# A hybrid decoder layer on one core: both projections by Strassen's identity, features in two halves, partial sums in DRAM

## The chip, the cores and the metric

The kernel runs on one core of a Trainium2 chip. The metric is the device time of one execution in microseconds, lower is better; a profiled execution also leaves a trace of every instruction on the core's engines: TensorE (PE, with its weight loads PEld), VectorE (DVE), ScalarE (ACT), GpSimd (POOL) and SyncE (SP), which issues nearly all DMAs.

## The reference

One layer over 1024 tokens of 2048 features, all in float32, batch 1:

```python
mod = silu(c) @ w_ada + b_ada                    # (2048) x (2048, 6144)
shift, scale, gate = split(mod, 3)
h = rms_norm(x, norm_gain) * (1 + scale) + shift
proj = h @ w_in                                  # (1024, 2048) x (2048, 8192)
q_sb, k_sb, v_sb, z_sb, q_r, k_r, v_r, z_r = split(proj, 8)   # 1024 columns each
# eight heads of 128: stick-breaking attention, strictly causal
qa, ka = rms_norm(q, q_gain), rms_norm(k, k_gain)             # per head
beta = sigmoid(qa . ka / sqrt(128))
A[t, s] = beta[t, s] * prod_{s < j < t} (1 - beta[t, j])
oa = (A @ v) * silu(z_sb)
# eight heads of 128: retention in chunks of 128 tokens
o[t] = sum_{s <= t} gamma_h ** (t - s) (rot(q_t) . rot(k_s)) v_s
ob = group_norm(o) * ret_gain * silu(z_r)
out = x + gate * (concat(oa, ob) @ w_out)        # (1024, 2048) x (2048, 2048)
```

The two projections are nearly all of the arithmetic.

## The kernel before

A float32 operand of a projection is split into two parts, a high one that TensorE's faster fp32r format holds exactly (ACT copy) and the rest (VectorE subtraction, line 121 for weights). A product of two operands is three matmuls (`mm3`, lines 132 to 135): high x high, low x high, high x low. PE's order is the program's (`manual_schedule`, line 61); the other engines' and the DMA queue's order is set by a scheduler, by priority and estimated readiness.

**Start (lines 218 to 450).** x is loaded by blocks of 128 tokens, scaled by its rows' root mean squares and transposed on PE. Sums of silu(c) w_ada run in chunks of 256 columns (`ada_sums`, line 273), on VectorE, ACT and POOL. The scale's chunks come first, the shift's later: until then h.T stands without its shift, and from that the z columns of seven retention heads are projected (`start_mm`) and spilled to DRAM; the shift's share in them is added later (`z_bias`, line 508).

**Input projection.** h.T stays in SBUF as 16 blocks of features by two halves of tokens, in two parts. `unit_t` (line 139) takes 128 columns of w_in: 16 blocks x 2 halves x 3 matmuls, 128 weights x 512 tokens, accumulated over all features in a PSUM bank a half. `unit_v` (line 156) takes 256 columns of values with h as the stationary operand: 256-wide matmuls whose result stands by tokens, as the heads need it. Weights are streamed in 256 KB tiles (`wchunk`, line 124).

**Heads.** The heads are tasks whose small products stand between the steps of the projection (`steady` calls `tick` after each six matmuls; a task says how many steps it waits). `qk_norm` (line 539) takes q and k from SBUF and works out their norms as 512-wide tiles with three Newton iterations (lines 556 to 561). `sb_attention` (line 581) takes blocks of 128 queries by 512 keys: sigmoids on ACT (619, 620), masks on POOL (622, 624), a running product on VectorE (632), a product (636), transposes on PE (649), splits (663, 664), products with the values. `ret_attention` (line 797): rotation of q and k (788 to 795), states (816, 822), scores (829, 831), values with their statistics (842 to 859), transposes and gating (866 to 872). Head outputs go to DRAM (`concat`).

**Output projection (`out_unit`, line 749).** Four groups of 512 columns of w_out over all 16 blocks of features, tokens in PSUM's partitions; the first group by halves of tokens while the last head ends. `finish` (line 940) multiplies by the gate and adds x (951, 952). The gate's sums run on VectorE during the retention heads (`gate_part`, line 484).

Of the kernel before, what the change touches and what calls it, by code (L numbers as in the profile page):

```python
# [29 lines left out]
SB_GAP = 3  # L30
NORM_GAP = 3
NORM_GAP2 = 6
SPLIT_GAP = 2
ZT = 1
BE = 3
TURN = 2
TURN_PRIO = 400
RT_ONE = False
ZB_GAP = 2
K0_WAIT = 8  # L40
NZ = 7
ADA_BUFS = 9
ADA_ACT = (2, 4, 7, 9, 12, 14)
SHIFT_GAP = 6
X_LOAD = {3: (4,), 5: (5,), 7: (6,), 8: (7,)}
X_STAT = {5: (4,), 7: (5,), 9: (6,), 10: (7,)}
X_TURN = 10
MOD_AT = 4
ENG = mybir.EngineType
MANUAL = (ENG.PE,)  # L50
LO_POOL = ()
RT_GAP = 5
# [3 lines left out]
def layer_kernel(ctx, tc, x, c, w_ada, b_ada, norm_gain, w_in, sb_q_gain, sb_k_gain, ret_norm_gain, w_out,  # L56
# [12 lines left out]
    concat = [dr.tile([P, S], F32, name=f"concat{f}") for f in range(KC)]  # L69
    gate_row = dr.tile([1, D], F32, name="gate_row")  # L70

# [1 line left out]
    ident = cons.tile([P, P], F32, name="ident")  # L73
    make_identity(nc, ident)
    ones = cons.tile([P, 32], F32, name="ones")
    nc.vector.memset(ones, 1.0)
    mean_r = cons.tile([P, P], F32R, name="mean_r")
    nc.vector.memset(mean_r.bitcast(F32), 1.0 / HD)

    c_sb = hp.tile([P, HALF], F32, tag="hl14_1", name="c_sb")[:, 0:16]  # L80
# [3 lines left out]

# [4 lines left out]
    cols = cons.tile([P, 58], F32, name="cols")  # L89
    rows = hp.tile([P, HALF], F32, tag="hl15_1", name="rows")  # L90
    nc.vector.memset(rows[:, 0:P], 0.0)
    nc.scalar.dma_start(rows[0:16, 0:P], norm_gain.rearrange("o (k p) -> (o k) p", p=P))
    nc.scalar.dma_start(rows[16:48, 0:P], b_ada[:, 0:2 * D].rearrange("o (k p) -> (o k) p", p=P))
    nc.scalar.dma_start(rows[48:49, 0:P], sb_q_gain)
    nc.scalar.dma_start(rows[49:50, 0:P], sb_k_gain)
    nc.scalar.dma_start(rows[50:58, 0:P], ret_norm_gain.rearrange("o (k p) -> (o k) p", p=P))
    rows_ps = ps.tile([P, P], F32, tag="C", name="rows_ps")
    nc.tensor.transpose(rows_ps, rows[:, 0:P], ident)
    nc.vector.tensor_copy(cols, rows_ps[:, 0:58])
    gain_c = cols[:, 0:16]  # L100
    shift_b = cols[:, 16:32]
    qg = cons.tile([P, 1], F32, name="qg")
    nc.vector.tensor_scalar(qg, cols[:, 48:49], 1.0 / math.sqrt(HD), None, op0=ALU.mult)
    kg = cols[:, 49:50]
    ret_g = cols[:, 50:58]

    def rsqrt_newton(y, m, u, iters=3):
        """y = m ** -0.5 from the exponent trick and Newton's iteration (u is room for a product)."""
        nc.vector.tensor_scalar(y.bitcast(I32), m.bitcast(I32), -0.5, RSQRT_MAGIC, op0=ALU.mult, op1=ALU.add)
        for _ in range(iters):  # L110
            nc.vector.tensor_tensor(u, y, y, op=ALU.mult)
            nc.vector.scalar_tensor_tensor(u, u, -0.5, m, op0=ALU.mult, op1=ALU.mult)
            nc.vector.scalar_tensor_tensor(y, u, 1.5, y, op0=ALU.add, op1=ALU.mult)

# [1 line left out]
    def split_w(raw, name, lo_eng=nc.vector):  # L116
        n = raw.shape[1]
        hi = wp.tile([P, HALF], F32R, tag="wh", name=f"wh_{name}")
        nc.scalar.activation(hi[:, 0:n], raw, AF.Copy)  # L119
        lo = wp.tile([P, HALF], F32R, tag="wl", name=f"wl_{name}")  # L120
        lo_eng.tensor_tensor(lo[:, 0:n], raw, hi[:, 0:n].bitcast(F32), op=ALU.subtract)  # L121
        return hi, lo

    def wchunk(parts, name, lo_eng=nc.vector):
        raw = wp.tile([P, HALF], F32, tag="wr", bufs=3, name=f"wr_{name}")
        for dst, src in parts(raw):
            nc.sync.dma_start(dst, src)
        return split_w(raw, name, lo_eng)

    w_in_k = w_in[0].rearrange("(k p) n -> p k n", p=P)  # L130

    def mm3(o, a_hi, a_lo, b_hi, b_lo, first, last):
        nc.tensor.matmul(o, a_hi, b_hi, start=first, stop=False)  # L133
        nc.tensor.matmul(o, a_hi, b_lo, start=False, stop=False)  # L134
        nc.tensor.matmul(o, a_lo, b_hi, start=False, stop=last)  # L135

    h_hi, h_lo = {}, {}  # by block of 128 features and half of the tokens

    def unit_t(col0, halves, name, lo_pool=()):
        """(w_in[:, col0:col0+128]).T @ h.T, 512 tokens a bank. Yields between its steps; returns the banks."""  # L140
        o = {hf: ps.tile([P, HALF], F32, tag="pj", bufs=4, name=f"pj_{name}_{hf}") for hf in halves}
        for kq in range(4):
            def parts(raw):
                yield raw.rearrange("p (k n) -> p k n", n=P), w_in_k[:, 4 * kq:4 * kq + 4, col0:col0 + P]
            with tc.high_priority(AHEAD):
                hi, lo = wchunk(parts, f"{name}_{kq}", nc.gpsimd if kq in lo_pool else nc.vector)
            for hf in halves:
                for k in range(4):
                    kc = 4 * kq + k
                    sl = slice(k * P, (k + 1) * P)  # L150
                    mm3(o[hf], hi[:, sl], lo[:, sl], h_hi[kc, hf], h_lo[kc, hf], kc == 0, kc == KC - 1)
                    if k % 2:
                        yield
        return o

    def unit_v(col0, name):
        """h @ w_in[:, col0:col0+256]: two heads' values, two blocks of tokens a bank."""
# [853 lines left out]
```

## Time and profile before

| | |
|---|---|
| device time, median of 3 | 2157.0 us (2154.09 to 2159.65) |
| span of the profiled execution | 2156.7 us |
| mean granted TensorE clock | 0.989 |
| PE / DVE / ACT / POOL busy | 2066.9 / 1212.4 / 744.9 / 340.0 us |
| DMA | 224.29 MB, mean 104 GB/s |

The page of the profile gives busy time by engine, forty slices of the span with the busy share in tenths, the chain of work that ended last, and groups of equal instructions with `xcount | busy us, mean ns | idle time before them and what ended it`. Matmuls are pipelined, so the mean durations of back-to-back ones overlap. A row of the windows gives, for a stretch, the busy time and instruction count of each engine, the granted clock, the DMA engines' share and GB/s. The profiled execution's own time is its span.

### The profile page before, as it was taken

To read this page: it belongs to the slowest core of one execution; us is meant where nothing else is said; L and a number is where in the kernel's file an instruction comes from. 1 tells how busy PE (TensorE), PEld (TensorE's weight loads), DVE (VectorE), ACT (ScalarE), POOL (GpSimd) and SP (SyncE) were. 2 spreads that over 40 slices of the span, in tenths; PEclk is the share of its full clock that TensorE was granted. 3 is DMA by queue.
4 is the path that set the end of the run, shared out by engine and by line. 5 is a ranking of instruction groups with operands and counts; after the bars stand their busy time and mean duration, and the time that the engine had idled before them with its cause. 6 is when DMAs were issued, how large, how long until landed. Compare 5 with 4: busy or idle time off the path is not lost.

```text
span 2156.7 us, 29735 instructions
## 1 busy us (share of the span) xinstructions
PE 2066.9 (96%) x11167; PEld 1771.6 (82%) x11167; DVE 1212.4 (56%) x2270; ACT 744.9 (35%) x1424; POOL 340.0 (16%) x475
## 2 busy tenths in 40 slices
PE   4878899999999999999999999999999999999998
PEld 3656779888988898888988988988988988688887
DVE  6999774477448653865386556556355146523132
ACT  6655442444235433543254222223232123311110
POOL 3654330111011201120111101011011010000000
PEclk9989999999999999999999999999999999999999
DMA  8847511221222112121212533433232124734132
GB/s 281 297 153 231 181 49 59 79 69 45 64 69 74 50 59 74 56 62 59 74 50 77 168 117 96 132 97 115 89 96 62 54 62 146 223 104 132 49 127 78
DMA packets 232404, 224.29 MB, mean 104 GB/s; under 512 B 12674, under 2 KB 187844, under 8 KB 232260
## 3 DMA queue, kind: packets, MB, share of 16 engines
q1 hardware_dynamic: 231872, 222.36, 32.8%
q8 instruction: 87, 1.43, 0.3%
q14 instruction: 57, 0.47, 0.1%
q10 hardware_dynamic: 388, 0.04, 0.0%
HBM read 194.03 MB, written 28.32 MB: 103 GB/s over the span
## 4 chain that ended last, share of the span: by engine, by line
PE 73%; DVE 13%; DMA 5%; issue 4%; ACT 3%; POOL 1%; ACTq 0%; SPq 0%; DVEq 0%; POOLq 0%
PE y L134 4%; PE y L135 4%; PE y L133 4%; PE pv_v L135 3%; PE pv_v L134 3%; PE pv_v L133 3%; PE pj_rq L133 3%; PE pj_rq L135 3%; PE pj_rq L134 3%; PE pj_rk L133 3%; PE pj_rk L135 3%; PE pj_rk L134 3%; PE pj_q L134 2%; PE pj_z L133 2%; PE pj_q L133 2%
## 5 line engine op out<-in xcount | busy, mean ns | idle before, releaser
L133 PE MATMUL pv_rv<-wh_rv,h_hi 128*128 128x256 f32 x512 | 146.5, 286 | 3.5 <-ACT wh_rv L119 3.5
L133 PE MATMUL y<-wh_o,c_hi 128*128 128x512 f32 x384 | 149.4, 389 | 0.0
L134 PE MATMUL y<-wl_o,c_hi 128*128 128x512 f32 x384 | 149.4, 389 | 0.0
L135 PE MATMUL y<-wh_o,c_lo 128*128 128x512 f32 x384 | 149.4, 389 | 0.0
L134 PE MATMUL pv_rv<-wl_rv,h_hi 128*128 128x256 f32 x512 | 146.1, 285 | 0.8 <-DVE wl_rv L121 0.7
L134 PE MATMUL pv_v<-wl_v,h_hi 128*128 128x256 f32 x512 | 144.9, 283 | 0.0
L133 PE MATMUL pv_v<-wh_v,h_hi 128*128 128x256 f32 x512 | 144.9, 283 | 0.0
L135 PE MATMUL pv_rv<-wh_rv,h_lo 128*128 128x256 f32 x480 | 136.4, 284 | 0.0
L135 PE MATMUL pv_v<-wh_v,h_lo 128*128 128x256 f32 x480 | 135.8, 283 | 0.0
L121 DVE TENSOR_TENSOR wl_o<-wr_o,wh_o 128x512 fp32r<-128x512 f32 x48 | 33.2, 692 | 180.3 <-ACT wh_o L119 180.3
L632 DVE TENSOR_TENSOR_SCAN om<-om 128x128 f32<-128x128 f32 (+2 forms) x96 | 96.2, 1002 | 43.6 <-POOL om L622 42.3
L119 ACT ACTIVATE wh_o<-wr_o 128x512 fp32r<-128x512 f32 x48 | 30.3, 632 | 220.7 <-PE y L135 216.3
L133 PEld LDWEIGHTS pv_rv<-wh_rv,h_hi 128*128 128x128 f32 x512 | 98.8, 193 | 4.9 <-ACT wh_rv L119 3.9
L133 PE MATMUL pj_rq<-h_hi,wh_rq 128*128 128x512 f32 x256 | 102.6, 401 | 0.3 <-ACT v L469 0.3
L133 PE MATMUL pj_rk<-h_hi,wh_rk 128*128 128x512 f32 x256 | 102.3, 400 | 0.0
L283 POOL TENSOR_TENSOR acc_p<-acc_p,ada 128x256 f32<-128x256 f32 x96 | 87.0, 907 | 96.9 <-ACT ada L282 68.0
L133 PE MATMUL pj_z<-h_hi,wh_z 128*128 128x512 f32 x256 | 101.3, 396 | 0.0
L133 PE MATMUL pj_q<-h_hi,wh_q 128*128 128x512 f32 x256 | 100.7, 393 | 0.0
L135 PE MATMUL pj_q<-h_hi,wl_q 128*128 128x512 f32 x256 | 100.6, 393 | 0.0
L134 PEld LDWEIGHTS pv_rv<-wl_rv,h_hi 128*128 128x128 f32 x512 | 98.9, 193 | 1.8 <-DVE wl_rv L121 1.6
L133 PE MATMUL pj_k<-h_hi,wh_k 128*128 128x512 f32 x256 | 100.2, 392 | 0.0
L135 PE MATMUL pj_rq<-h_hi,wl_rq 128*128 128x512 f32 x256 | 100.1, 391 | 0.0
(273 smaller groups left out, 5820.9 us busy)
## 6 DMA issues: line engine op xcount, KB each, us to landing
ada<-in_w_ada_dram SPq DMA_DIRECT2D x64, 512.0 KB
gr<-in_w_ada_dram SPq DMA_DIRECT2D x64, 256.0 KB
wr_o<-in_w_out_dram SPq DMA_DIRECT2D x48, 256.0 KB
x<-in_x_dram SPq DMA_DIRECT2D x32, 256.0 KB
wr_rz<-in_w_in_dram SPq DMA_DIRECT2D x32, 256.0 KB
wr_q<-in_w_in_dram SPq DMA_DIRECT2D x32, 256.0 KB
wr_k<-in_w_in_dram SPq DMA_DIRECT2D x32, 256.0 KB
wr_z<-in_w_in_dram SPq DMA_DIRECT2D x32, 256.0 KB
```

The source lines that it names most:

```text
L119: nc.scalar.activation(hi[:, 0:n], raw, AF.Copy)
L121: lo_eng.tensor_tensor(lo[:, 0:n], raw, hi[:, 0:n].bitcast(F32), op=ALU.subtract)
L133: nc.tensor.matmul(o, a_hi, b_hi, start=first, stop=False)
L134: nc.tensor.matmul(o, a_hi, b_lo, start=False, stop=False)
L135: nc.tensor.matmul(o, a_lo, b_hi, start=False, stop=last)
L283: nc.gpsimd.tensor_tensor(acc_p, acc_p, src, op=ALU.add)
L632: nc.vector.tensor_tensor_scan(rev, rev, rev, init, op0=ALU.mult, op1=ALU.bypass)
```

## The change

The new program splits tokens, features and columns in halves of pairs of blocks and takes Strassen's identity in Winograd's form: seven products of half-size blocks instead of eight, with sums of blocks ahead and behind. Names: A11, A12, A21, A22 are the left blocks (two halves of tokens by even and odd feature blocks), `S1` to `S4` their sums, the right blocks are B11 to B22 of the weights.

- Left operands: only half the features (8 of 16 blocks) are in SBUF at a time, as four pairs of blocks; for each of the seven combinations there are four tiles in two parts (`place`). The second half of h.T is held in DRAM (`xs`) and replaces the first at the end of the first stream (`gather`, `swap`).
- A `Group` is 256 columns by half the features: two loads of 512 KB, four sums of weights on VectorE, seven splits, seven products of 4 blocks x 3 matmuls (128 weights x 512 tokens), all with tokens along the width, values too. P1, P6, P5 and P3 accumulate in one bank, P7 and P4 in a second, P2 stands in a third; between them ACT copies the bank (`copied`) and VectorE adds (`added`).
- The input projection runs as two streams of 32 groups: the first half of the features, with partial sums written to DRAM (`part`), then the second half, which adds the loaded partial sums on POOL (line 237) or VectorE and writes the results to DRAM (`fin`). The output projection likewise: features of the stick-breaking heads, then of the retention heads (`ypart`).
- P3 and P4 of a group stand behind the first product of the next.
- Heads take q, k, v, z from DRAM. Values are transposed on PE (`turn_v`). The norm's means are worked out over 256 tokens at a time through single-buffered tiles, written to DRAM as a row, read back one number a token, and applied in the sigmoids' scale (q) and as a broadcast row (k).
- The stick-breaking heads run in the second input stream, the retention heads from its end into the first output stream. Head outputs go to DRAM; `mix_sums` makes S1 to S4 of them on POOL, and `take` loads the left tiles of the next stream behind the last use of the old ones, calling `tick` until the mixed tiles are written.
- All of w_ada is summed on VectorE: four blocks of scale and shift before the first product, the other four and the gate as a task in the first stream. The z columns need no later bias.
- The output is transposed back on PE (128 transposes) and added to x.

```diff
-    def unit_t(col0, halves, name, lo_pool=()):
-    def unit_v(col0, name):
...
+    def combine(a11, a12, a21, a22, new, sub):
+        s1, s2, s4 = (new(n) for n in ("S1", "S2", "S4"))
+        sub.tensor_tensor(s1, a21, a22, op=ALU.add)
+        sub.tensor_tensor(s2, s1, a11, op=ALU.subtract)
+        sub.tensor_tensor(a21, a11, a21, op=ALU.subtract)
+        sub.tensor_tensor(s4, a12, s2, op=ALU.subtract)
+        return {"A11": a11, "S3": a21, "S2": s2, "A12": a12, "S1": s1, "S4": s4, "A22": a22}
...
+        def product(self, p, bank, first):
+            with tc.high_priority(AHEAD):
+                src = self.right(p)
+                hi = wp.tile([P, NP, P], F32R, tag="wh", bufs=3, name=f"wh_{self.name}_{p}")
+                lo = wp.tile([P, NP, P], F32R, tag="wl", bufs=3, name=f"wl_{self.name}_{p}")
+                split(hi, lo, src)
+            for j in range(NP):
+                a_hi, a_lo = left[LEFT[p], j]
+                mm3(bank, hi[:, j, :], lo[:, j, :], a_hi, a_lo, first and j == 0, j == NP - 1)
+                if j % 2:
+                    yield
...
+    def copied(g, src, i, hf, name):
+        t = pp.tile([P, HALF], F32, tag="pt", bufs=PT, name=f"{name}_{g.name}")
+        gt = g.gate[i]
+        nc.scalar.activation(t, src, AF.Copy, scale=1.0 if gt is None else gt)
+        if g.seed is not None:
+            nc.gpsimd.tensor_tensor(t, t, old(g, i, hf), op=ALU.add)
+        return t
...
+        def second_half():
+            for j in range(NP, 2 * NP):
+                acc = yield from ada_sums(k1, "sg", NSG, "sg", (D + 256 * j, 256 * j), f"a{j}", 4)
+                yield 4
+                ada_mod(j, acc)
+            for i in range(4):
+                acc = yield from ada_sums(k1, "sg", NSG, "sg", (2 * D + 512 * i, 2 * D + 512 * i + 256), f"g{i}", 4)
+                yield 4
+                mod = over_partitions(acc, f"g{i}")
...
+        run(stream([Group(w_in_k, 0, 256 * i, f"e{i}", put=to_dram(part, 2 * i)) for i in range(32)], gather))
...
+    def qk_norm(h, pool):
+        for i, b in enumerate((h, NH + h)):
+            for qt in range(4):
+                sl = slice(qt * 256, (qt + 1) * 256)
+                sq = pool.tile([P, 256], F32, tag="n0", name=f"sq_{b}_{qt}")
+                nc.sync.dma_start(sq, fin[b][:, sl])
+                nc.scalar.activation(sq, sq, AF.Square)
+                shi = pool.tile([P, 256], F32R, tag="n1", name=f"shi_{b}_{qt}")
+                slo = pool.tile([P, 256], F32R, tag="n2", name=f"slo_{b}_{qt}")
+                split(shi, slo, sq)
+                yield PRO_GAP
+                ms = ps.tile([P, 256], F32, tag="A0", name=f"ms_{b}_{qt}")
+                nc.tensor.matmul(ms, mean_r, shi, start=True, stop=False)
+                nc.tensor.matmul(ms, mean_r, slo, start=False, stop=True)
+                row = pool.tile([P, 256], F32, tag="n0", name=f"row_{b}_{qt}")
+                nc.scalar.activation(row[0:1, :], ms[0:1, :], AF.Identity, bias=eps_c[0:1, :])
+                nc.sync.dma_start(msq[h][i:i + 1, sl], row[0:1, :])
...
+    def take(g):
+        def tell(n):
+            for j in range(NP):
+                while f"mix{g}_{j}" not in ready:
+                    tick()
+                    switch()
+                place(n, j, loaded(mix[g][j][n], f"c{g}_{n}_{j}"))
+        return tell
+
+    run2(stream(second, take(0)))
+    run2(stream([Group(w_out_k, 0, 256 * i, f"y{i}", gate=gates[2 * i:2 * i + 2], put=to_dram(ypart, 2 * i))
+                 for i in range(8)], take(1)))
+    drain()
...
+        run(stream([Group(w_out_k, 8, 256 * i, f"o{i}", seed=ypart[2 * i:2 * i + 2], gate=gates[2 * i:2 * i + 2],
+                          put=put_y(i), done=lambda i=i: start(finish(i), 2)) for i in range(8)]))
```

The prediction calls the four streams first (e), second (f), first output (y) and second output (o).

1216 lines of the change are left out of this document (541 added, 675 removed).

## The prediction

> **What bounds the kernel now.** I read the page first: busy shares, slices, the chain that ended last.
>
> ```profile
> span 2156.7 us, 29735 instructions
> PE 2066.9 (96%) x11167; PEld 1771.6 (82%) x11167; DVE 1212.4 (56%) x2270; ACT 744.9 (35%) x1424; POOL 340.0 (16%) x475
> ...
> PE   4878899999999999999999999999999999999998
> DVE  6999774477448653865386556556355146523132
> ...
> PE 73%; DVE 13%; DMA 5%; issue 4%; ACT 3%; POOL 1%; ACTq 0%; SPq 0%; DVEq 0%; POOLq 0%
> ```
>
> TensorE is busy 96% of the span and in every slice but the first five; the chain is 73% PE. VectorE (DVE) is the next engine, 56% on average but 6 to 9 tenths early on. Only fewer or shorter products can make this kernel much faster, as long as nothing that feeds them becomes later. Second, four stretches (PE, PEld, DVE, ACT and POOL busy with instruction counts, granted clock, DMA share, GB/s):
>
> ```profile
> 0.00:300.00 300.00, 232.05 (x982) 183.89 (x983) 246.90 (x437) 165.81 (x350) 139.69 (x141) 0.93 0.65 210
> 0.00:60.00 60.00, 30.00 (x129) 24.04 (x130) 42.63 (x97) 37.88 (x88) 24.46 (x33) 0.94 0.88 285
> 180.00:260.00 80.00, 68.59 (x287) 55.69 (x288) 71.71 (x109) 38.00 (x74) 35.74 (x37) 0.91 0.65 205
> 300.00:1180.00 880.00, 874.84 (x4950) 762.15 (x4950) 525.00 (x857) 358.26 (x698) 123.01 (x284) 1.00 0.20 63
> ```
>
> The start moves 285 GB/s and is held by DMA; around 200 us VectorE is 90% busy and PE waits (granted clock 0.91); the heads' 880 us run with PE 99% busy while VectorE has 525 us of work. This room on VectorE, 355 us, is what the change spends. Third, the timeline, for the pace of back-to-back products, since the mean durations in the groups overlap:
>
> ```profile
> 1507.33 0.28 PE L134 MATMUL pv_rv<-wl_rv,h_hi 128*128 128x256 f32 x1
> 1507.69 0.28 PE L134 MATMUL pv_rv<-wl_rv,h_hi 128*128 128x256 f32 x1
> 1509.10 0.39 PE L842 MATMUL op<-v,pT 128*128 128x128 f32 x2
> 1509.55 0.39 PE L842 MATMUL op<-v,pT 128*128 128x128 f32 x2
> ...
> 2140.07 0.39 PE L133 MATMUL y<-wh_o,c_hi 128*128 128x512 f32 x1
> 2140.75 0.39 PE L133 MATMUL y<-wh_o,c_hi 128*128 128x512 f32 x1
> ```
>
> Three products of width 512 take 0.68 us (2140.07 to 2140.75), 0.227 each; three of width 256 take 0.36, 0.12 each; four 128-wide f32 products (two rows of x2) take 0.45, 0.112 each. Rates and durations are of one execution, whose span of 2156.7 us stands 0.3 us under the median of 2157.0, so I sum against the median without a correction.
>
> **What goes and comes on TensorE.** Counts are from the two programs. Before: 6144 projection products of width 512 (six input kinds x 768, output 1536) and 3072 of width 256 (values): 1394 + 369 = 1763 us. After: 80 groups x 7 products x 12 = 6720 of width 512, 1525 us. That is 238 us less, 11%. Added: 128 transposes of values and 128 of the output, 29 us. The heads' own products stay (110 us for scores and values, 88 for 128-wide ones, 14 for the norms' means). By these rates before needs 1975 us; of the other 181, some 100 lie in the first 300 us (982 products in the first row, at about 0.2 each), 10 behind the last product, and 70, 4% of the rest, are switches between kinds of product and short waits. So without new waits after would take about 1950. I now go through its five stages for what feeds TensorE, whose order is written out and strict: a product that waits holds all projection behind it.
>
> **Start, 116 us.** Before starts to project with the first block's scale alone. After needs four of eight blocks of scale and shift before any product. In its DMA order come 2 MB of weights, 8.4 of x, 4.2 out to DRAM, 16.8 of w_ada: 31.5 MB at 285 GB/s are 110 us. Behind the last block stand its sums, the scaling and splits (6 us, partly under the first product).
>
> **First stream, 32 groups, 688 us.** 32 x 84 x 0.227 = 610 us, with means 613. Its first 36 products (98 us) contain all remaining matmuls of the conditioning, scale and shift and the gate, each waiting for 4.2 MB; 33.6 MB with the weights and partial sums of that time make 44 MB, 154 us at 285 GB/s, 176 at 250. I take 65 us of wait (56 to 78). VectorE's price there:
>
> ```profile
> L121 DVE TENSOR_TENSOR wl_o<-wr_o,wh_o 128x512 fp32r<-128x512 f32 x48 | 33.2, 692 | 180.3 <-ACT wh_o L119 180.3
> L521 DVE SCALAR_TENSOR_TENSOR zb_acc<-zw,shift,zb_acc 128x512 f32<-128x512 f32 x15 | 11.2, 747 | 6.0 <-DMA zw<-in_w_in_dram 5.9
> L119 ACT ACTIVATE wh_o<-wr_o 128x512 fp32r<-128x512 f32 x48 | 30.3, 632 | 220.7 <-PE y L135 216.3 <-PE y_0b L135 3.6 <-DVE wl_o0b L121 0.7
> ```
>
> 128 sums at 0.747 (L521's form) and five groups at 9.7 give 144 us, so both press. Later a group is light: per 19.0 us of PE, VectorE has 7 splits, 4 sums of weights and 3 additions at 0.692 (9.7 us), ACT 7 splits and 3 copies at 0.63 (6.3). 10 us for switches.
>
> **Second stream, 32 groups and the stick-breaking heads, 950 us.** PE by the rates 782 us, with 4% for switches 811. VectorE: 32 x 15 x 0.692 = 332, eight groups' SiLU 22, one and a half retention heads 33, and the heads. In the stretch 300 to 1180 above they cost 525 less 136 splits of weights (94), 431. The norm is now a few numbers a token; its old iterations go:
>
> ```profile
> L560 DVE SCALAR_TENSOR_TENSOR y_q<-u_q,y_q 128x512 f32<-128x512 f32 x48 | 42.1, 878 | 0.5
> L559 DVE SCALAR_TENSOR_TENSOR u_q<-u_q,m_q 128x512 f32<-128x512 f32 x48 | 33.0, 687 | 19.8 <-ACT u_q L558 19.4
> ```
>
> These are the first and the last of four rows (q and k, 142 us together); new small splits and factors add about 55. Sum: 332 + 22 + 33 + 431 - 142 + 55 = 731 at most; form by form I get 709. That is 90% of PE, and POOL comes on top: 96 additions of old partial sums, 16 mixed sums.
>
> ```profile
> 1304.04 1.80 POOL L793 TENSOR_TENSOR sw_k<-sw_k,sin 128x512 f32<-128x512 f32 x1 [2.33 <-DVE ga L496]
> 1304.65 1.73 DVE L121 TENSOR_TENSOR wl_rq<-wr_rq,wh_rq 128x512 fp32r<-128x512 f32 x1
> ```
>
> At 1304.65 a split of 0.69 takes 1.73 us; it ends only after POOL's product, which lasts to 1305.84. If every POOL operation (213 us at 1.8) delayed VectorE fully, VectorE would need 922 us; if none, 709.
> The Trainium skill, "SBUF — State Buffer", section "SBUF: two separate sides", calls the shared port pair "an exclusive lock, not a bandwidth split", and says that it hits VectorE with two SBUF inputs. By that rule the additions from PSUM are spared, and I estimate 840; by the row alone it could be 922. Either is near PE's 811, and the trace agrees with the full block.
>
> The tighter part is the new norm. For 64 quarters it runs a ring through one buffer: PE mean, ACT row, row to DRAM, the next quarter loaded into the same buffer, square, split, PE mean again. PE waits at each mean, and behind it all projection. Nearest rows:
>
> ```profile
> L620 ACT ACTIVATE be<-zp 128x256 f32<-128x256 f32 x16 | 6.3, 391 | 0.0
> 1344.39 0.37 ACT L503 ACTIVATE grow<-gp 1x256 f32<-1x256 f32 x1 [7.85 <-PE gp L501]
> 1344.79 0.25 SPq L504 DMA_DIRECT2D gate_row<-grow  x1
> 1346.02 0.35 DVE L494 TENSOR_SCALAR ga<-gr,silu_c 128x256 f32<-128x256 f32 x1 [6.93 <-DMA gate_row<-grow]
> ...
> 1346.92 0.37 SPq L127 DMA_DIRECT2D wr_rv<-in_w_in_dram  x1
> ...
> 1349.72 0.63 ACT L119 ACTIVATE wh_rv<-wr_rv 128x512 fp32r<-128x512 f32 x1 [4.96 <-DMA wr_rv<-in_w_in_dram]
> ```
>
> A row of 0.37; a 1 KB write frees its buffer after 1.23 us (1344.79 to 1346.02); a 256 KB load takes 2.8 to its user (1346.92 to 1349.72). The 128 KB load is not shown: 1.2 to 2.8, I take 2.0, as it has half the bytes. Square and split 0.39 each, VectorE's half 0.42, matmuls and issue 0.8: 5.6 us with nothing in the way. ACT (504 of 811 us by the same counting) and VectorE (90%) will be in the way four times, and the in-order DMA queue puts stores and loads that wait for POOL or VectorE between write and load, so 7 to 11; I take 8.8. The products between two means take 5.4 us bare and 6 to 9 with a head's step: over the 63 spacings the excess is 32 us for a ring of 7, 74 for 8, 125 for 9, 181 for 10, 237 for 11. For 8.8: 115. The first head also waits some 12 us for its norms through DRAM, and 12 go to full VectorE queues. 811 + 115 + 12 + 12 = 950.
>
> **First output stream and the drain, 302 us.** The order of products shows retention heads 4 to 7 in one row behind the first product of the last group (behind it the new left operands wait for the mixed tiles): no projection covers them. On VectorE a head costs
>
> ```profile
> L822 DVE SCALAR_TENSOR_TENSOR state<-state,up 128x128 f32<-128x128 f32 x48 | 13.7, 285 | 15.7 <-PE up L816 14.6
> L848 DVE BATCH_NORM_STATS2 st<-op 128x6 f32<-128x128 f32 x64 | 14.3, 279 | 0.2 <-PE op L844 0.2
> L858 DVE TENSOR_SCALAR on<-op,mv,y 128x128 f32<-128x128 f32 x64 | 22.4, 404 | 0.5
> L111 DVE TENSOR_TENSOR u<-y 128x4 f32<-128x4 f32 x48 | 7.7, 161 | 1.3
> L795 DVE TENSOR_TENSOR rk<-rk,sw_k 128x512 f32<-128x512 f32 x16 | 17.5, 1091 | 12.0 <-POOL sw_k L793 11.8
> ```
>
> 7 x 0.285 + 8 x 0.279 + 8 short ones + 8 x 0.404 + 20 x 0.161 + 8 of rotation (0.69 to 1.09) + 4 of 0.7 to 0.75, 22 us; transposes, ACT copies and loads between them 8 more. Before, this lay under projections. Head 4's rest 27 and three heads at 30 are about 115 us, of which 28 are PE's own in its 193 for this stage: 87 added. Gaps of 4 steps (5.4 us) where a head's statistics need 5.5 plus queue add 14, switches 8.
>
> **Second output stream, 190 us.** PE 167, swapping left tiles through three buffers 8, switches 3, last additions, transposes and stores 12.
>
> Sum: 116 + 688 + 950 + 302 + 190 = 2246 us. The 210 us saved on TensorE are more than used up by four stretches in which nothing covers a wait: 65 + 115 + 87, and the start.
>
> **Rivals.**
> *Short ring (faster).* The ring stays under 7 us since ACT and VectorE serve it at once, and POOL's lock falls on idle time: second stream 855, first 672 at full DMA rate, 290 and 186 behind, start 112: 2115. For it: PE is 99% busy over 880 us while VectorE has 60%; against it: 90% here, as in the stretch 180 to 260, where PE lost 14%. The ring alone brings the sum to 2157 at 6.8 us.
> *Blocked DMA queue.* Stores that wait for VectorE stand ahead of the ring's write and load every time: 11 us, 237 in place of 115: 2368. For it: in the program's DMA order up to a dozen entries lie between a quarter and the next; against it: most are ready early.
> *Clock.* With waits every 8 us the second stream could be granted 0.91, as in 180 to 260, for 811 / 0.91, 80 us more: 2326. Against it: waits here are shorter.
> The Trainium skill, "TensorE: Matmul & The Clock Gate", section "Part 1: The HAM clock gate", halves the clock after an idle window of about 3.4 us; by it waits of 1 to 4 us would rarely count, and the drain would, where TensorE isn't the bound. The trace's 0.91 with gaps agrees in kind.
>
> That the products don't shrink is excluded by the count, 6720.
>
> **Chances.** Forecast 0.45 (own range 2165 to 2300), short ring 0.26, blocked queue 0.17, clock 0.12. Faster by over 0.3% (under 2150, about what a measurement can tell) 0.22, within it 0.04, both from the short ring; slower 0.74. The range 2120 to 2390 leaves out half the short ring's lower side and a blocked queue beyond 11 us.
>
> **What would show it.** Products in the second half of the first stream 0.227 us apart with PE over 95%; waits of PE for the conditioning's sums in the first 270 us of about 65 us; waits at the norms' means near 100 us, with the quarter's load or split as releaser; a stretch of about 115 us with PE a quarter busy near the end of the first output stream; 512-wide projection products 6720. I am wrong if PE is over 95% busy through the second stream (then the ring is short), or if VectorE alone ends its waits, with no DMA in the ring's chain.

## The result and the profile after

The changed kernel takes 2554.4 us (median of 4 runs, 2546.4 to 2559.2), the kernel before 2156.0 (4 runs, 2154.1 to 2159.7): a ratio of 1.184, 95% interval 1.182 to 1.187. The forecast was 2246 with a range to 2390. So the direction was right, but the time lies 164 us above the range's upper end, and 308 us above the forecast. The profiled execution of the changed kernel took 2550.4 us, its span is 2548.4.

The page of the changed kernel (busy time and share of each engine; busy tenths of TensorE and tenths of the granted clock, in 40 slices of 64 us):

```profile
span 2548.4 us, 28539 instructions
...
PE 1998.8 (78%) x9121; PEld 1637.6 (64%) x9121; DVE 1532.6 (60%) x2749; ACT 946.1 (37%) x1754; POOL 401.5 (16%) x494
...
PE   3255669999999996888886878979867697646798
...
PEclk8668789999999998899998988989978898758899
```

TensorE was busy 96% of the span before and now is 78%. Its busy time fell by 68 us only, though about 210 us of products went. The row of the clock says why: in every slice in which PE is at 7 tenths or below, the clock is at 8 or below. By the trace's clock records it stood at half for 551 us of this span (before: 51), and TensorE was busy for 264 us of that time (before: 42). At half pace up to 132 of the 264 us are lost (before: 21), an estimate; that would be some 110 of the 140 us by which its busy time fell short of the products saved.

A second view gives the five stages, cut at the first product of each stream (columns: length; busy time and instructions of PE, PEld, DVE, ACT, POOL; granted clock; DMA share; GB/s):

```profile
0.00:138.20 138.20, 40.47 (x290) 39.26 (x290) 86.24 (x168) 64.28 (x134) 19.29 (x18) 0.73 0.71 229
138.20:882.90 744.70, 652.42 (x2753) 535.05 (x2754) 415.68 (x619) 236.71 (x406) 32.97 (x20) 0.92 0.45 141
882.90:1959.50 1076.60, 868.92 (x4033) 705.77 (x4032) 700.49 (x1221) 477.78 (x943) 248.01 (x381) 0.91 0.49 155
1959.50:2338.80 379.30, 265.65 (x1250) 217.91 (x1249) 217.30 (x574) 106.35 (x174) 68.26 (x51) 0.82 0.47 152
2338.80:2548.40 209.60, 171.38 (x801) 139.56 (x799) 112.91 (x168) 60.99 (x99) 33.02 (x24) 0.93 0.57 181
```

Against the terms of the forecast. "Idle" sums TensorE's idle times of over 0.03 us. "Half pace" sums, over neighbouring 512-wide products that begin 0.26 to 0.6 us apart while the granted clock is 0.5, what each takes beyond 0.227; narrow products at half clock come on top.

| stage | forecast | measured | idle | half pace |
|---|---|---|---|---|
| start | 116 | 138.2 | 97.7 | – |
| first stream | 688 | 744.7 | 92.3 | 25.1 |
| second stream | 950 | 1076.6 | 207.6 | 33.7 |
| first output stream | 302 | 379.3 | 113.6 | 9.8 |
| second output stream | 190 | 209.6 | 33.3 | 2.0 |
| sum | 2246 | 2548.4 | 544.5 | 70.6 |

What ended TensorE's idle time over the whole span (total us, times, longest):

```profile
PE vtp L524 <- DMA vT<-fin: 111.2, 13, 20.9
PE mod_m L346 <- DVE acc_a L338: 84.2, 6, 20.8
PE otp L798 <- DVE on L790: 61.5, 17, 8.5
PE ms L546 <- ACT shi L117: 61.1, 30, 9.9
PE mod_g L346 <- DVE acc_g L338: 39.4, 4, 11.4
PE ms L547 <- DVE slo L118: 28.9, 30, 2.7
...
PE b_o L121 <- ACT p_o L235: 26.9, 1, 26.9
PE zp L121 <- ACT R L117: 18.3, 1, 18.3
```

The forecast knew mod (conditioning), ms (norm means), otp (the drain) and zp (first head). It did not know the largest row, the transposes of v that wait for v's load. The row of b_o, 26.9 us, is the swap of the left tiles ahead of the last stream, which it had at 8 us; its lines stand in the section on the prediction.

The timeline of TensorE around one conditioning sum in the first stream shows that such a wait is paid a second time (start, duration, engine, line, tiles, form, count, idle time before):

```profile
198.71 0.39 PE L123 MATMUL b_e<-S_h,wl_e_P 128*128 128x512 f32 x1
208.13 1.84 PE L346 MATMUL mod_m<-ones,acc_a 128*128 128x1 f32 x8 [9.03 <-DVE acc_a L338]
...
210.40 0.63 PE L122 MATMUL b_e<-A_l,wh_e_P 128*128 128x512 f32 x1
210.83 0.63 PE L123 MATMUL b_e<-A_h,wl_e_P 128*128 128x512 f32 x1
...
215.57 0.39 PE L121 MATMUL b_e<-S_h,wh_e_P 128*128 128x512 f32 x1
215.80 0.39 PE L122 MATMUL b_e<-S_l,wh_e_P 128*128 128x512 f32 x1
```

After 9.03 us of waiting, products begin 0.427 us apart (210.40 to 210.83) in place of 0.227, until about 214.6; only then are they back at full pace.

The last view is SyncE's queue ahead of the longest wait for v, at 1866.9 (start, time to issue, line, the transfer):

```profile
1845.84 0.44 SPq L710 DMA_DIRECT2D q0r<-fin  x1
1848.10 0.32 SPq L506 DMA_DIRECT2D mix_S<-mA  x1
1851.07 0.32 SPq L509 DMA_DIRECT2D mix_S<-mA  x1
...
1857.91 0.33 SPq L512 DMA_DIRECT2D mix_S<-mA  x1
...
1862.77 0.33 SPq L712 DMA_DIRECT2D k0c<-in_rot_dram  x1
1863.14 0.90 SPq L495 DMA_DIRECT2D vT<-fin  x2
```

The loads of v (1863.14) stand behind the loads of the rotation, which wait for buffers, and behind four stores of mixed tiles, which wait 1.7 to 2.9 us each for POOL. TensorE stood still from 1845.9 to 1866.9.

### The profile page after: what moved, and what is told of

Read it like the earlier page. It is cut to its first block, busy times and chain, and to the rows that moved or that the text cites. A ratio compares the mean times of both kernels' runs of the same rounds, so it can differ in the third digit from the quotient of the medians.

```text
span 2548.4 us, 28539 instructions
## 1 busy us (share of the span) xinstructions
PE 1998.8 (78%) x9121; PEld 1637.6 (64%) x9121; DVE 1532.6 (60%) x2749; ACT 946.1 (37%) x1754; POOL 401.5 (16%) x494
## 5 line engine op out<-in xcount | busy, mean ns | idle before, releaser
L121 PE MATMUL b_f<-S_h,wh_f_P 128*128 128x512 f32 x384 | 156.8, 408 | 1.2 <-ACT u_f L235 1.2
L121 PE MATMUL b_e<-S_h,wh_e_P 128*128 128x512 f32 x384 | 154.1, 401 | 2.6 <-ACT u_e L235 1.7
L122 PE MATMUL b_f<-S_l,wh_f_P 128*128 128x512 f32 x384 | 155.8, 406 | 0.0
L123 PE MATMUL b_f<-S_h,wl_f_P 128*128 128x512 f32 x384 | 155.7, 406 | 0.0
L122 PE MATMUL b_e<-S_l,wh_e_P 128*128 128x512 f32 x384 | 152.8, 398 | 0.0
L123 PE MATMUL b_e<-S_h,wl_e_P 128*128 128x512 f32 x384 | 152.6, 397 | 0.0
L237 POOL TENSOR_TENSOR u_f<-u_f,cp_f 128x512 f32<-128x512 f32 x64 | 86.6, 1352 | 322.8 <-ACT u_f L235 309.6
L118 DVE TENSOR_TENSOR wl_f_P<-wr_f,wh_f_P 128x512 fp32r<-128x512 f32 x128 | 100.0, 781 | 40.3 <-ACT wh_f_P L117 40.0
L118 DVE TENSOR_TENSOR wl_e_P<-wr_e,wh_e_P 128x512 fp32r<-128x512 f32 x128 | 89.4, 698 | 46.5 <-ACT wh_e_P L117 46.3
L338 DVE SCALAR_TENSOR_TENSOR acc_a<-ada_a,silu_c,acc_a 128x512 f32<-128x512 f32 x120 | 90.7, 759 | 25.6 <-DMA ada_a<-in_w_ada_dram 22.9
```

The costliest lines, as they stand in the source:

```text
L118: nc.vector.tensor_tensor(lo, src, hi.bitcast(F32), op=ALU.subtract)
L121: nc.tensor.matmul(o, a_hi, b_hi, start=first, stop=False, skip_group_check=True)
L122: nc.tensor.matmul(o, a_hi, b_lo, start=False, stop=False, skip_group_check=True)
L123: nc.tensor.matmul(o, a_lo, b_hi, start=False, stop=last, skip_group_check=True)
L237: nc.gpsimd.tensor_tensor(t, t, old(g, i, hf), op=ALU.add)
L338: nc.vector.scalar_tensor_tensor(acc, src, cj, acc, op0=ALU.mult, op1=ALU.add)
```

## Experiments

All are edits of the changed kernel unless said otherwise; each ratio is to the kernel before, run on the same chip. "Less" and "more" are against the 2554.4 us of the changed kernel; the kernel before took 2155.4 to 2157.2 beside these runs, so some 2 us of a difference may be the chip's. *Theory A*, with which I went in: the missing time is waits for loads that the one in-order DMA queue issues late, and the half clock after each wait. *Theory B*: VectorE together with POOL bounds the second stream.

**The norm's ring.** The next quarter is loaded a step earlier into a second buffer, and the row of means gets its own; the differences T1 and T2 of the weights have two buffers in place of three to pay for it.

```diff
...
+            after = fetch(0)
             for qt in range(4):
-                sq = pool.tile([P, 256], F32, tag="n0", ...)
-                nc.sync.dma_start(sq, fin[b][:, sl])
+                sq, after = after, fetch(qt + 1) if qt < 3 else None
...
-                row = pool.tile([P, 256], F32, tag="n0", ...)
+                row = pool.tile([P, 256], F32, tag="n3", ...)
```

> One edit to the changed kernel: in the norms of q and k the quarter of squares for the next step is loaded one step earlier, and the row of means has a buffer of its own (paid for by two buffers in place of three for the right-hand differences T1 and T2). Theory A (waits for loads that the one in-order DMA queue of SyncE issues late, each followed by a few us of products at half pace): the waits of TensorE for shi and slo, 96 us in 64 steps of the changed kernel, fall under 30 us, and the time falls by 60 to 100 us, to 2455 to 2495. Theory B (VectorE with POOL is the bound of the second stream): the same time is waited elsewhere, and the time stays within 15 us of 2554.

Measured 2441.8 us, ratio 1.133 (1.130 to 1.136): 113 us less. Its second stream as a stretch, then the waits of TensorE in it at v and at the means:

```profile
877.10:1859.50 982.40, 831.03 (x4034) 689.41 (x4033) 722.05 (x1224) 465.24 (x947) 267.01 (x381) 0.93 0.54 171
```

```profile
PE vtp L524 <- DMA vT<-fin: 70.9, 7, 22.8
...
PE ms L551 <- ACT be L610: 11.1, 10, 2.5
```

The waits for shi and slo are gone, and what is left at the means is 11.1 us. PE's busy time in the stream also fell, from 869 to 831, with the same products (clock 0.91 to 0.93). VectorE did not become the bound: the fall is more than Theory A asked for, and Theory B fell here.

**v loaded early.** The two loads of v go out at the head's start, in the retention heads ahead of the rotation.

```diff
         nc.sync.dma_start(dm, ret_mask[h])
+        raws = load_v(6 * NH + h, ...)          # two buffers of its own
         rotated(rt, 4 * NH + h, q, f"q{h}")
...
-            turn_v(6 * NH, h, v, None, hf, "BC"[hf])
+            turn_v(6 * NH, h, v, None, hf, "BC"[hf], raws[hf])
```

> One edit to the changed kernel: the two loads of v for a head's transposes are issued at the head's start, before the loads of the rotation in the retention heads, in buffers of their own there. Theory A: vtp waits for vT (111 us, 13 times) fall under 35 us; in the retention heads part of it comes back as a wait of ktp for the rotated k, which is next late; the time falls by 30 to 90 us. Theory B: the sum of TensorE's waits stays, and the time is within 10 us of 2554.

Measured 2491.4 us, ratio 1.156 (1.154 to 1.159): 63 us less. TensorE's waits in it:

```profile
PE ktp L748 <- DVE r L723: 18.0, 1, 18.0
...
PE vtp L529 <- DMA vT<-fin: 14.0, 3, 11.0
```

111 us of waits for v became 14, and 18 came back as the wait for the rotated k of the first retention head, as Theory A said.

**Conditioning from another queue.** The 256 loads of w_ada in the first stream are issued by POOL.

```diff
-                nc.sync.dma_start(src[:, i * 256:(i + 1) * 256], ada_rows[:, j, col:col + 256])
+                q.dma_start(src[:, i * 256:(i + 1) * 256], ada_rows[:, j, col:col + 256])    # q = nc.gpsimd
```

> One edit to the changed kernel: in the first stream the 256 loads of w_ada go out from POOL's queue, no longer from SyncE's behind the stores of partial sums. Theory A: from 138 to 400 us the rate rises from 200 GB/s to 260 or more, the eight waits for the conditioning sums (about 80 us in the first stream) fall under 40 us, the products at half pace after them get fewer, and the time falls by 35 to 65 us. Rival (the rate itself or VectorE's sums bound this stretch, the queue's order does not): the waits stay within 15 us of what they were. The issuing of a load by POOL has no row yet; if it takes over 1 us each, the loads come slower and the time rises by up to 50 us.

Measured 2536.3 us, ratio 1.176 (1.173 to 1.178): 18 us less, a miss. POOL's timeline in it:

```profile
159.54 7.92 POOL L333 DMA_DIRECT2D ada_a<-in_w_ada_dram  x15
```

POOL needs 0.53 us to issue one (7.92 for 15), 17 us for the 32 loads of a sum, where 11 us of products lie between two sums: even if they landed at once, the loads would leave some 6 us of wait a sum. From 140 to 400 us the rate was 209 GB/s, hardly over the 200 of the changed kernel and far from the 260 asked for, and the waits for the sums fell from 81.5 to 63.6 us only. So this run leaves open how much of the waits the queue's order was.

**Conditioning spread out.** The same loads on SyncE, three steps after each four, not one.

```diff
             if every and j % every == every - 1:
-                yield 1
+                yield 3
```

> One edit to the changed kernel: in the first stream the conditioning task yields 3 steps after every four loads, no longer 1, so that its eight sums are spread over 16 steps each (22 us of products) and not 8 (11 us). Theory A: a step's 4.2 MB need some 20 us at the 200 GB/s of this stretch, so the waits for the sums (about 80 us in the first stream) fall under 20 us and most of the half-paced products (26 us) go with them; the first stream takes 640 to 680 us instead of 745 and the time falls by 60 to 100 us. Rival (the stores and loads queued on SyncE hold the sums whatever their spacing): the first stream stays above 710 us.

Measured 2501.1 us, ratio 1.159 (1.157 to 1.161): 53 us less. The first stream as a stretch, then its waits for the sums:

```profile
138.20:822.20 684.00, 645.42 (x2754) 529.25 (x2755) 409.79 (x619) 236.84 (x406) 33.66 (x20) 0.96 0.48 154
```

```profile
PE mod_m L346 <- DVE acc_a L338: 13.9, 3, 6.4
PE mod_g L346 <- DVE acc_g L338: 12.3, 4, 4.3
```

744.7 us became 684.0, 4 above the expected band, and the 53 us are 7 short of theirs; idle time fell from 92 to 39. That the spacing was too short for the loads is shown, as they stayed on the same queue. But some 29 us of waits for the sums are left, above the 20 asked for, and the half-paced products stayed nearly whole (22 us for 25). One of them in the timeline, and two stretches of 3.4 us behind it:

```profile
241.48 0.39 PE L123 MATMUL b_e<-S_h,wl_e_P 128*128 128x512 f32 x1
244.02 1.02 PE L346 MATMUL mod_m<-ones,acc_a 128*128 128x1 f32 x8 [2.15 <-DVE acc_a L338]
...
246.34 0.63 PE L122 MATMUL d_e<-A_l,wh_e_P 128*128 128x512 f32 x1
246.77 0.63 PE L123 MATMUL d_e<-A_h,wl_e_P 128*128 128x512 f32 x1
```

```profile
245.40:248.80 3.40, 3.40 (x9) 2.65 (x9) 1.67 (x5) 0.00 (x0) 0.00 (x0) 0.50 0.93 331
248.80:252.20 3.40, 3.40 (x16) 2.79 (x16) 2.65 (x4) 0.83 (x2) 0.00 (x0) 1.00 0.36 98
```

A wait of 2.15 us and the 1.02 us of narrow products behind it are enough for a window of 3.4 us at half clock: 9 products in it, 16 in the next.

**Filling the waits with useless products.** Ahead of each conditioning sum in the first stream, products of a resident operand into two banks that nobody reads; first 40, then 52 a sum.

```diff
+            for tag in ("A0", "A1"):
+                idle = ps.tile([P, HALF], F32, tag=tag, ...)
+                for i in range(20):          # then 26
+                    nc.tensor.matmul(idle, a[:, 0:P], a, start=i == 0, stop=i == 19, ...)
         mod = ps.tile([P, 4], F32, tag="C", name=f"mod_{name}")
```

> The changed kernel with work added: ahead of each of the eight conditioning sums that TensorE waits for in the first stream (9 to 11 us each) stand 40 products of 512 columns whose result nobody reads, 320 in all, 73 us at 0.227 us each. Theory A (a wait of several us costs a second time, since the products after it run at half pace for 4 to 5 us): the added products fill the wait, the products after it stay 0.227 us apart, and the time falls by 10 to 25 us although 73 us of work are added. Rival (the half pace has another cause, the load or the transfers of this stretch): the time stays or rises by up to 20 us.

Measured 2553.9 us, ratio 1.184 (1.181 to 1.187): no change, though 73 us of work were added. The waits shrank (idle in the first stream 92 to 31), but 1.5 to 4.3 us were left in seven of eight places, and each was followed by half pace. The expected gain of 10 to 25 us did not come, and the time alone is the rival's; so the next run fills the waits to their end.

> The kernel with products that nobody reads ahead of the eight conditioning sums, 52 each in place of 40, so that they outlast the waits (9 to 11.6 us): 94 us of added work in all. With 40 a wait of 1.5 to 4 us was left, and a window of 3.4 or 6.8 us at half pace followed in seven of eight places. Theory A (a wait of over about 2 us is what halves the clock): with waits under 1 us the windows go, the half-paced products of the first stream cost under 10 us in place of 26, and the first stream takes 725 to 740 us against 745, 5 to 20 us less for 94 us more work. Rival (the narrow products of the sums themselves halve it): the windows stay, and the time rises by up to 15 us.

Measured 2537.8 us, ratio 1.177 (1.175 to 1.179): 17 us *less* for 94 us *more* work. The first stream:

```profile
139.10:871.10 732.00, 720.41 (x3169) 594.18 (x3170) 414.01 (x619) 236.57 (x406) 32.85 (x20) 0.99 0.45 144
```

The clock is 0.99 in place of 0.92, and half pace costs 7 us in place of 25. The same narrow products of the sums stand there, so they alone do not halve the clock; it takes the wait ahead of them. It is the clearest sign of a wait's second price.

**Half the spacing of the retention heads.** `RT_GAP = 2` in place of 4.

> One constant of the changed kernel: a step of a retention head every 2 ticks in place of 4, so that more of heads 4 to 7 lies under the products of the first output stream. Theory A: the stretch at its end in which TensorE is half idle (140 us) shrinks to 50 to 90 us and the time falls by 40 to 80 us. Theory B (a head's chain of VectorE and DMA steps sets its pace, whatever its spacing in the program): each wait inside a head grows by what the stretch loses, and the time stays within 20 us.

Measured 2548.5 us, ratio 1.183 (1.181 to 1.185): 6 us less, hardly beyond the spread. Second and first output stream:

```profile
882.80:1991.20 1108.40, 891.70 (x4106) 723.03 (x4105) 718.62 (x1284) 481.77 (x950) 254.33 (x385) 0.90 0.48 154
1991.20:2343.40 352.20, 248.41 (x1178) 202.86 (x1177) 201.33 (x510) 102.09 (x167) 63.72 (x47) 0.83 0.47 153
```

What the output stream gains (27 us) the second stream loses (32). Theory A's reading was wrong: writing the heads closer together moves work from one stream to the other and removes hardly any wait. The time is Theory B's; that waits inside the heads grew is not shown (vtp 111 and 106 us, otp 62 and 64).

**POOL's additions left out** (the partial sums are loaded but not added there).

```diff
-            nc.gpsimd.tensor_tensor(t, t, old(g, i, hf), op=ALU.add)
+            old(g, i, hf)
```

> This kernel leaves out part of the sum: the partial sums of the first halves are loaded but not added by POOL (three quarters of the blocks of the second stream and of the second output stream). Theory A (waits for loads and what follows them): the time falls by less than 30 us, most of it from the wait for the first output block (27 us). Theory B (VectorE and POOL, which hold each other up, bound the second stream): the second stream falls by 60 us or more.

Measured 2521.9 us, ratio 1.170 (1.167 to 1.172): 33 us less, and 32 of them lie in the second stream:

```profile
885.40:1930.00 1044.60, 862.18 (x4033) 700.62 (x4032) 663.12 (x1223) 479.50 (x945) 118.25 (x285) 0.92 0.50 159
```

VectorE's busy time falls from 700 to 663 us with the same work, so POOL does hold it up, by 37 us. The gain in the second stream is half of what Theory B asked for. Theory A's account is wrong too: it looked for the gain at the first output block, whose wait stayed (27.3 us, 26.9 with POOL's additions).

**The streams alone, after and before.** In both kernels the heads are left out and the gates z stand for their outputs.

> This kernel leaves out the heads: norms, scores, weights, values and retention; the gates z take the place of the heads' outputs, so that the four streams, their combinations and their transfers remain. Forecast's terms for the streams alone: second stream 609 us of products, first output stream 153 and its combination of the head pairs. Theory A: the second stream then runs at 0.227 us a product and takes 610 to 650 us, the first output stream 165 to 215, the whole 1880 to 1990 us. Theory B (evacuation of the seven products on VectorE, ScalarE and POOL bounds the streams themselves): the second stream stays above 700 us.

> The kernel before, with the same parts left out as in the changed kernel without heads (norms, scores, weights, values, rotation and retention; the gates z take the place of the heads' outputs). The heads' products take about 221 us of TensorE there, and TensorE waits 75 us in all. Theory C (TensorE is so full before that its heads cost about their own products, and the seven-product streams by themselves gain little, since their start, conditioning and hand-overs take back what the saved products give): 1900 to 1970 us, so that the streams alone are within 50 us of the changed kernel's 1919. Rival (the streams alone gain the 210 us of products, and all of the loss is in the heads): 2080 us or more.

After without heads 1919.2 us, ratio 0.890 (0.889 to 0.891); before without heads 1912.3 us, ratio 0.887 (0.886 to 0.888). After's second stream took 671 us, between the two theories (610 to 650, over 700); both whole times lie in the expected bands. The two pages' rows of busy time, after and then before:

```profile
PE 1652.5 (86%) x7201; PEld 1359.7 (71%) x7201; DVE 1065.3 (56%) x1621; ACT 642.3 (33%) x1114; POOL 263.5 (14%) x190
```

```profile
PE 1827.0 (96%) x9439; PEld 1557.5 (82%) x9439; DVE 623.2 (33%) x1030; ACT 450.3 (24%) x832; POOL 138.3 (7%) x139
```

This is the result that I learned most from. Seven products for eight take 174 us from TensorE's busy time, and the streams by themselves are still no faster. The change loses the whole saving before a single head runs: after starts its first projection product at 140 us (before: 37), waits 91 us in its first stream, 43 in its second, 24 in its last. And the heads, which cost 2155 − 1912 = 243 us before (their own products, taken start to start in its trace, are 221 us), cost 2554 − 1919 = 635 after.

**Three edits together**: the ring, v, and the spread conditioning.

> Three edits to the changed kernel together: squares loaded one step early with the row in its own buffer (alone it took 113 us), v loaded early (63 us), conditioning spread over 16 steps a sum (53 us). If the three waits are separate, the gains add: 2554 less 229 is 2325, so 2305 to 2350 us; still slower than before. If they stand in for one another (one bound behind all three), it stays above 2390 us.

Measured 2308.9 us, ratio 1.071 (1.069 to 1.072): 246 us less, 17 more than the sum of the three. So the waits are separate, and the gains add. It is still 153 us slower than before.

**Spacings on top of the three edits.** Heads stepped twice as fast (stick-breaking every tick, retention every 2); then with norms every 2 ticks too; then retention alone; then norms alone.

> The three edits together, and a stick-breaking head steps every tick in place of every second, a retention head every 2 in place of 4. Theory A (with the loads early, the spacing sets the pace): the stick-breaking heads end earlier, the retention heads start earlier and the stretch without stream products at the end of the first output stream shrinks, 2230 to 2290 us. Theory B (the chain inside a head sets its pace): TensorE's waits inside the heads grow by what the stretch loses, and the time stays within 20 us of the three edits alone.

> The three edits, the heads stepped twice as fast, and the norms stepped every 2 ticks in place of 4. Theory N (with fast heads the norms are what a head waits for: its q and k can then be loaded and split only at its own start, 17 to 25 us of exposed chain a head, eight times): the wait of zp for R falls from 161 us to under 50, the retention heads start earlier, the first output stream stays near 204 us, and the time is 2190 to 2270 us. Rival (VectorE's and POOL's work in the heads is the pace): the wait moves to another tile of the heads, and the time stays above 2300 us.

> The three edits, and of the two spacings only that of the retention heads halved. Theory N: the retention heads do no harm; the time is 2280 to 2312 us, at most that of the three edits (2309). Rival (the faster retention heads did the harm of 93 us): above 2350 us.

> The three edits, and of the spacings only that of the norms halved. Theory N: with the heads at their old pace the norms were ahead of them already from the third head on, so the time stays within 25 us of 2309. Rival (the norms pace the heads in either case): it falls by 40 us or more.

| spacing (heads, retention, norms) | us | ratio, 95% | second + first output stream |
|---|---|---|---|
| 2, 4, 4 (three edits) | 2308.9 | 1.071 (1.069–1.072) | 951 + 327 |
| 1, 2, 4 | 2401.5 | 1.114 (1.112–1.115) | 1180 + 204 |
| 1, 2, 2 | 2340.6 | 1.086 (1.083–1.088) | 1101 + 220 |
| 2, 2, 4 | 2303.7 | 1.068 (1.067–1.070) | 978 + 299 |
| 2, 4, 2 | 2343.4 | 1.087 (1.085–1.089) | 945 + 369 |

With 1, 2, 4 every head waits for its split q and k, since the norms come too late to load them under the head before:

```profile
PE zp L121 <- ACT R L117: 160.7, 8, 25.1
```

With norms every 2 ticks that row is gone, as expected, but the time comes to 2340.6 and not under 2270: the waits of the other tiles (otp 56, vtp 40, tp_B 19) are there, and the clock in the second stream is 0.93. 2, 4, 2 missed too, 34 us slower. No spacing tried brings the two streams together under 1277 us. 2, 2, 4 is within 6 us of the three edits, as expected: the faster retention heads alone do no harm, so what 1, 2, 4 loses comes with the faster stick-breaking heads. It is the best of all and still 147 us slower than before; no run here points to a spacing that would beat the kernel before.

## Why the prediction was right in sign and wrong in size

- **Right: products 0.227 us apart and PE over 95% busy in the second half of the first stream.** From 400 to 883 us:

```profile
400.00:883.00 483.00, 477.48 (x2095) 394.49 (x2094) 250.44 (x370) 173.18 (x301) 15.41 (x8) 0.99 0.34 110
```

- **Right in place, near in size: the norm's means.** Forecast 115 us in the second stream, with the load or split as releaser. The trace has 61.1 + 28.9 us for shi and slo and 5.8 for ACT's be, 96; the edit to the ring takes back 113, more than the waits themselves. That the rest is the half clock behind them is not shown by itself. So *Short ring* was wrong: no run has the second stream over 95% busy. So was *Blocked DMA queue* as a story of the ring, for which it had 237 us.
- **Mis-sized: the start,** 138 for 116. The term took the 285 GB/s of before's first 60 us for the whole 31.5 MB; the stage ran at 229 GB/s, and 31.5 MB / 229 is 138. DMA alone did not set that rate: SyncE's loads of w_ada waited 24.5 us there for buffers that VectorE's sums had to free.
- **Mis-sized: the conditioning.** Forecast 65 us of waits; 81.5 are there in the first stream (mod_g 39.4, mod_m 29.0 and 13.1), and 25 of half pace behind them. The spacing was too short for this rate: 61 us of the stage went when the sums were spread.
- **Mis-sized: the first output stream,** 379 for 302. The drain took 140 us and not 115:

```profile
2182.00:2322.00 140.00, 72.01 (x330) 59.36 (x331) 77.00 (x253) 22.74 (x36) 28.72 (x23) 0.67 0.37 121
```

  TensorE is half busy at a clock of 0.67, where the forecast counted the heads at full clock and TensorE a quarter busy. And v's loads waited here too: 51 of the 111 us lie in this stream.
- **Mis-sized: the swap of left tiles ahead of the last stream,** 27 us for 8. It goes through three buffers, as forecast, but one operation behind the other on ACT:

```profile
2346.03 1.27 ACT L117 ACTIVATE S_h<-c_S 128x512 fp32r<-128x512 f32 x2 [2.08 <-DMA c_S<-mix_S]
...
2369.05 0.63 ACT L117 ACTIVATE A_h<-c_A 128x512 fp32r<-128x512 f32 x1 [0.85 <-DMA c_A<-mix_A]
2370.50 0.69 ACT L235 ACTIVATE p_o<-b_o,gate_c 128x512 f32<-128x512 f32 x1 [0.82 <-DVE A_l L118]
```

  Some 20 splits of new left tiles, most of them waiting for their load, stand on ACT ahead of the copy p_o that empties the PSUM bank b_o. TensorE stands still until that copy. POOL is not in this chain: without its additions the wait is 27.3 us. This is read from the trace; no run moved the copy ahead.
- **Failed step: the sum holds no wait for v, and no half clock.** "811 + 115 + 12 + 12 = 950" counted TensorE at full clock and let the in-order queue touch the ring alone. In its place the second stream has 60 us of waits for v (59.9 of 207.6 idle) and 34 us lost by 512-wide products at half pace. The queue was seen ("up to a dozen entries lie between a quarter and the next") but priced for one user; the largest wait was another's. *Clock* was written down with 0.91 for this stage, which is what was granted, but it got a chance of 0.12, as "waits here are shorter". And it was made an alternative to the forecast, priced for the second stream only. It is no alternative: it comes on top of the longer waits, and no stage was granted more than 0.93.
- **A premise that misled: "without new waits after would take about 1950".** It set the saved products against the whole kernel's time. The sum then did add waits to the streams themselves, but too few of them. The runs without heads show streams of nearly equal length, 1919 and 1912: the late start and the waits of the streams alone use up the saving, so nothing of it is left against the heads, which cost 392 us more than before (635 less 243).
- **VectorE and POOL.** Forecast 709 us of VectorE bare (87% of 811; the 90% fits its rough sum of 731) and 922 with full blocking; measured 700 with the blocking in it, of which 37 went with POOL's additions. So the bare count was too high, and the full blocking was far too high; what POOL's other operations add was not tested. The estimate of 840 that went with the Trainium skill ("SBUF — State Buffer", section "SBUF: two separate sides") is further off than the bare count; that POOL holds VectorE up at all agrees with it.

What stays open: with the three edits the heads still cost some 440 us (2309 less 1919 − 53, an estimate, as the streams were not run alone with these edits) against 243 before. Single waits of 60 us and less are named above, but no run removed them, and two retention heads side by side, or heads under other stages, were not tried.

## What to carry to other kernels

Price a saving stage by stage: take each stage alone, before and after, with its start and its waits, and only then add what runs beside it. On TensorE's in-order path most waits over 2 us are paid twice here, once as themselves and once in half-paced products behind them, so they add up to more than their rows. In a queue in order, ask for each load, not for one, which stores and buffer waits stand ahead of it; two loads at the head's start took back 63 us, one a step earlier (with a row's own buffer) 113.

## What the hardware showed beside this

**The half clock follows waits from about 2 us on, in a grain of 3.4.** I took every wait of TensorE of 0.3 us or more that stands alone (no other ends in the 7 us before it or begins in the 4 behind it; behind 140 us of the span; 15 profiles, the changed kernel and its variants) and looked whether the granted clock went to 0.5 between the wait's start and 3.5 us behind its end. It did so behind 0 of 158 waits under 1 us, 19 of 167 of 1 to 2 us, 62 of 84 of 2 to 3, 62 of 66 of 3 to 4, and all 210 of over 4. What follows the wait counts too: of the waits of 2 to 3 us, all 18 ahead of a conditioning sum's narrow products did it, 15 of 24 ahead of a mean's 256-wide ones, 4 of 10 ahead of 512-wide projection. So length alone is no sure threshold, and no run separates the two. The low stretches last 3.4, 6.8, 10.2, 13.7 us and more, nearly all whole multiples of 3.41. A wait of 2 to 3 us mostly costs one such window, some eight products at 0.427, 1.6 us.

The Trainium skill, "TensorE: Matmul & The Clock Gate", section "Part 1: The HAM clock gate", tells of an idle window of about 3.4 us. The grain agrees; that an idle time must last so long does not: here the clock also fell behind waits of 2 to 3 us, 4 of 10 of them with 512-wide products right behind. The sentence of the prediction that hung on it, that waits of 1 to 4 us would rarely count, was wrong above 2 us and right below (19 of 167).

**Issuing a DMA costs POOL 0.53 us** (the row of POOL's timeline above, 128 KB each), where SyncE issued loads of w_ada of the same size in 0.42 (median of 128 issues in the same run's start); 32 loads take POOL longer than the 11 us of products that were to hide them.
